# Another order of the passage to the up quads, a load of its own for the root's table, and two 128-column matmuls in place of one behind 512-column products

## The chip, the cores and the metric

The kernel runs on one core of a Trainium2 chip. A core has a matrix engine (TensorE, PE in the profile), a vector engine (VectorE, DVE), a scalar engine (ScalarE, ACT), GpSimd (POOL) and a sync engine (SP) whose queue issues transfers. The metric is the device time of one execution in microseconds, the median of several runs.

## The reference

One layer of a decoder with x of 512 tokens by 1024 (float32) and 256 memory tokens. Cut to what matters:

```python
h = rmsnorm(x, norm_mix_g)
proj = h @ w_in                       # 1024 x 9216
p_a, p_b, q, p_g = split(proj)
y_a = (gb * conv3(gc * v)) @ w_a_out
y_b = silu(layernorm(conv31(u * sigmoid(ug)))) @ w_b_out
y_c = attention(q, rmsnorm(mem) @ w_kv, 4 heads) @ w_att_out
g = sigmoid(p_g + b_gate)             # three gates
x = x + (g0 * y_a + g1 * y_b + g2 * y_c) @ w_o
h = rmsnorm(x, norm_ffn_g)
u = conv3(h @ w_up); gt, up = split(u)
x = x + (silu(gt) * up) @ w_down      # inner width 2816
return rmsnorm(x, norm_final_g)
```

## The kernel before

**Products.** Each factor in float32 is split into a high part and a low part of the type float32r, and a product is three matmuls: high by high, high by low, low by high. The high part is a copy on ACT (`whi` of a weight, line 481), the low part a subtraction on DVE (`wlo`, line 485).

**Quads.** The large projections are not multiplied block by block but as *quads*: two halves of the 512 tokens, two halves of the 1024 inputs, two groups of columns. Seven products of blocks, with sums and differences before and behind, stand in place of eight. The seven have the numbers 1 to 7. Each product is 24 matmuls of 256 columns (`multiply`, line 662). Its moving operand is one of seven forms of the activations, by `OPERAND`: b00, b10 and b11 are blocks themselves, t4 to t7 sums of blocks. A form is a pair of tiles, `fb00h` and `fb00l` for instance, of four 128 x 256 pieces. In form t4 the first three pieces lie in the tiles `ft4h` and `ft4l`, and the fourth in a tile of its own, `ft4x`, that starts at another offset in memory. Product 4 goes through the pieces in the order 0, 1, 2, 3 for the first 128 output columns and 3, 2, 1, 0 for the second, so the pieces of `ft4x` stand together.

The forms are made for three activations: "h" (the normed x, `high` and `low`, lines 582 and 587), "y" (the output of branch b before w_b_out, `y_parts`, lines 1367 and 1372, made in two halves e = 0 and 1) and "h2" (the normed x of the second half). A quad keeps its sums in PSUM banks "a", "b" and "c". They are read by the jobs r1 to r7 (lines 685 to 715): reads r1, r4, r5 and r6 are on ACT, r2, r3 and r7 on DVE. The read r4 of a quad is the last use of its bank "a".

**Other work of PE.** Between the quads stand products of 512 columns in the same three parts (`product`, lines 432 to 434): values, attention and its output, the merging of branches, wo, and the down projection. There are also transposes (128 columns, lines 1155 and 1756), sums by a column of ones (line 791) and rows (line 800).

**Order.** PE's order is written out by hand as a list `seq`. `beside` (line 1890 and on) says what goes behind which product of a quad: behind product 6 of gate (1, 1) the sums for the layer norm of branch b and a part of a merge, behind its product 7 the layer norm's rows (`pe_rows("v", ...)`) and the rest of the merge, and behind its product 3 the two quads "mq 0" and "mq 1" of w_b_out, product by product in turn. Then come the products of wo, "a b f c d e g" (seven again, in two halves i = 0, 1 each), with `pe_transpose_rows(i)` ahead of each half of "g". Then the 11 up quads, with the transposes of rows 2 and 3 between their first products, and the down projection.

The other engines' orders are made by a planner. Every piece of work is a `job` with an engine, a cost, jobs that must come before it and buffers that it takes; the tables `LATER` and `AHEAD` shift kinds of jobs in time. The planner has no job for the loading of an activation table on ACT. Where the function changes to one of another table, the load is put ahead of the activation that needs it (1.28 us each, lines 1325, 1492, 1743). Each engine then works in program order.

**From wo to the up quads.** When the last of wo's products for a row of 128 tokens is in PSUM, DVE adds it to x (`add_row`, line 1730). ACT squares the row (`row_square`, 1737) and takes the root (`row_root`, 1743). DVE takes the reciprocal and scales (`row_norm`, 1747 and 1748). PE transposes (1756), and ACT and DVE make the forms "h2". Rows 0 and 1 are finished by product "e" of wo, rows 2 and 3 by "g".

Of the kernel before, what the change touches and what calls it, by code (L numbers as in the profile page):

```python
# [8 lines left out]
F32 = mybir.dt.float32  # L9
F32R = mybir.dt.float32r  # L10
AF = mybir.ActivationFunctionType
ALU = mybir.AluOpType
# [304 lines left out]
def hybrid_block_kernel(  # L317
# [42 lines left out]
    def name(s):  # L360
        uid[0] += 1
        return f"{s}_{uid[0]}"
# [181 lines left out]
    def form_tile(act, key):  # L544

        n = 3 if key == "t4" else 4
        t = [forms.tile([P, n, HALF], F32R, tag=key + s, name=name("f" + key + s)) for s in "hl"]
        form[act, key] = [[x[:, k, :] for k in range(n)] for x in t]
        if key == "t4":
            gap = (256 - SHIFT) // 4  # L550
            last = forms.tile([P, gap + 2 * HALF], F32R, tag="t4x", name=name("ft4x"))
            for i in range(2):
                form[act, key][i].append(last[:, gap + i * HALF : gap + (i + 1) * HALF])
            form[act, key, "views"] = [[x, y[3]] for x, y in zip(t, form[act, key])]
        else:
            form[act, key, "views"] = [[x] for x in t]
        return form[act, key, "views"]
# [6 lines left out]
    def form_jobs(act, blk, ready, sources=()):  # L564
# [10 lines left out]

        def pieces(t, views):
            return [t] if len(views) == 1 else [t[:, :3, :], t[:, 3, :]]

        def high(key, src):
            hi = form_tile(act, key)[0]  # L580
            for h, x in zip(hi, pieces(src(), hi)):
                nc.scalar.copy(h, x)

        def low(key, src):
            hi, lo = form[act, key, "views"]
            for h, l, x in zip(hi, lo, pieces(src(), hi)):
                nc.vector.tensor_tensor(l, x, h.bitcast(F32), op=ALU.subtract)

# [24 lines left out]
    def quad_loads(q, w, col0, col1, by_dma=False, take=("wf",), after=(), lows=()):  # L613
# [34 lines left out]
        split_job((q, 4), r, 4, 256, [("ld", r)], lo_from=low(4, 1, 1))  # L648

    def multiply(q, f, act):  # L650
        if f in (1, 2, 5):
            make(("bank", q, BANK_OF[f]))
        ps = halves(("bank", q, BANK_OF[f]))
        (w_hi, w_lo), (hi, lo) = w_units.pop((q, f)), form[act, OPERAND[f]]
        for c in range(2):
            at = slice(c * P, (c + 1) * P)
            for i in range(4):
                k = 3 - i if f == 4 and c else i
                first = f in (1, 2, 5) and i == 0 and c == 0
                again = not (f in (1, 2, 5) and c == 0)  # L660
                for n, (w, a) in enumerate(((w_hi, hi), (w_hi, lo), (w_lo, hi))):
                    nc.tensor.matmul(  # L662
                        ps[:, c, :], w[:, k, at], a[k], start=first and n == 0,
                        stop=i == 3 and n == 2, skip_group_check=again,
                    )

# [685 lines left out]
    def y_parts(key, e, src, after, use):  # L1352
        last = next(f for f in OPERAND if OPERAND[f] == key)

        def pieces(views):

            if len(views) == 1:
                return [(slice(0, 2), views[0][:, 2 * e : 2 * e + 2, :])]
            if e == 0:
                return [(slice(0, 2), views[0][:, :2, :])]  # L1360
            return [(slice(0, 1), views[0][:, 2:3, :]), (slice(1, 2), views[1].unsqueeze(1))]

        def high():
            if e == 0:
                form_tile("y", key)
            for at, h in pieces(form["y", key, "views"][0]):
                nc.scalar.copy(h, src()[:, at, :])

        def low():
            hi, lo = form["y", key, "views"]  # L1370
            for (at, h), (_, l) in zip(pieces(hi), pieces(lo)):
                nc.vector.tensor_tensor(l, src()[:, at, :], h.bitcast(F32), op=ALU.subtract)  # L1372

        hk, lk = ("fh", "y", key, e), ("fl", "y", key, e)
        job(hk, "ACT", actv(512), high,
            after + [(("gate", 1, 1), last)] + ([("fh", "y", key, 0)] if e else []), use=use)
        job(lk, "DVE", dve(512), low, [hk], use=use)
        form_ready.setdefault(("y", key), []).append(lk)
        return lk
# [355 lines left out]
    def row_square(t):  # L1735
# [3 lines left out]
        )  # L1739

    def row_root(t):
        r = column(SS_X + t, 1)
        nc.scalar.activation(r, r, AF.Sqrt, bias=eps, scale=1.0 / D)
# [48 lines left out]
    for t in range(NT):  # L1792
# [4 lines left out]
            take=[(("xnorm", t), "sb")], use=[("x1", t)])  # L1797
        job(("xroot", t), "ACT", 0.3, lambda t=t: row_root(t), [("xsquare", t)])
        job(("xnorm", t), "DVE", 1.40, lambda t=t: row_norm(t),
# [72 lines left out]
    for do in (  # L1872
# [38 lines left out]
        (GATE[1, 1], 6): lambda: (  # L1911
            pe_squares("v", ("csq", 0), NT, SEQ, [("var", "fold")], SEQ), pe_merge(0, 3, (0,))),
        (GATE[1, 1], 7): lambda: (pe_rows("v", R_V, NT), pe_merge(0, 3, (1,))),
        (GATE[1, 1], 3): lambda: [
# [7 lines left out]
    for p in WO:  # L1922
        for i in range(2):
            if p == "g":
                pe_transpose_rows(i)
            pe_wo(p, i)

# [391 lines left out]
```

## Time and profile before

| | us |
|---|---|
| median of 3 runs | 934.01 (931.47 to 934.22) |
| the profiled execution | 931.92 |
| its span, from first to last instruction | 930.2 |
| PE busy | 915.1 (98%) |
| DVE busy | 848.1 (91%) |
| ACT busy | 686.0 (74%) |
| PE's waits with a named releaser, in sum | 6.8 |

The table is from the page of the profile. Engine times overlap, so they do not add up. A matmul's record is longer than the distance to the next one: the matmuls are pipelined, and what counts is from start to start. In the trace a row shows its start, its length, engine, line, operation, output and inputs (buffer numbers left out), and in brackets the idle time before it and what ended it. "x8" groups eight instructions in a row.

### The profile page before, as it was taken

What the parts mean: (1) busy time and instruction counts of PE and PEld (TensorE: products, weight loads), DVE (VectorE), ACT (ScalarE), POOL (GpSimd) and SP (SyncE); (2) the same over time, 40 slices, a digit from 0 to 9 for tenths busy, and PEclk for the clock granted to TensorE, in tenths of its full rate; (3) what the DMA queues carried; (4) which work ended last, traced back from release to release, by engine and by line L of the source; (5) the groups of instructions that cost most, each with busy time, mean ns of one, the idle gap of its engine ahead of it and who ended that gap; (6) DMA issues with size and microseconds to landing.
All of it is one profiled execution on the core that took longest, in us unless ns stands there. A gap on an engine that the chain in (4) does not pass through costs nothing.

```text
span 930.2 us, 17118 instructions
## 1 busy us (share of the span) xinstructions
PE 915.1 (98%) x6813; PEld 863.5 (93%) x6813; DVE 848.1 (91%) x976; ACT 686.0 (74%) x938; POOL 137.4 (15%) x165
## 2 busy tenths in 40 slices
PE   9999999999999999999999999999999999999996
PEld 8999999999889999999899897799999999988885
DVE  7998999999989999999886999797999889999986
ACT  8577988889978867878767983686766667765665
POOL 0121111000011111120101211111221111002300
PEclk9999999999999999999999999999999999999999
DMA  9999579745688898887868899889999886689952
GB/s 363 382 251 227 123 182 220 166 114 113 165 183 222 204 203 202 215 187 212 181 140 214 199 252 330 206 211 305 278 245 230 201 167 128 169 313 316 248 110 91
DMA packets 55952, 196.91 MB, mean 212 GB/s; under 512 B 6336, under 2 KB 6464, under 8 KB 55872
## 3 DMA queue, kind: packets, MB, share of 16 engines
q0 software_dynamic: 22608, 81.54, 48.4%
q1 hardware_dynamic: 32544, 113.23, 33.5%
q8 instruction: 53, 0.87, 0.4%
q10 hardware_dynamic: 720, 1.06, 0.3%
q14 instruction: 27, 0.22, 0.1%
HBM read 191.60 MB, written 4.19 MB: 211 GB/s over the span
## 4 chain that ended last, share of the span: by engine, by line
PE 83%; issue 7%; DMA 4%; DVE 3%; ACT 1%; POOL 1%; ACTq 0%; POOLq 0%; DVEq 0%
PE bank L662 55%; PE bank L432 6%; PE bank L434 6%; PE bank L433 5%; PE bank L1469 3%; PE bank L1467 3%; PE bank L1468 3%; PE bank L918 2%; DMA wo<-in_w_o 2%; DMA wf<-in_w_b_out 2%; DMA wf<-in_w_up 1%; DVE wlo L485 1%; ACT whi L481 0%; PE bank L1155 0%; POOL whol L502 0%
## 5 line engine op out<-in xcount | busy, mean ns | idle before, releaser
L481 ACT CAST whi<-wf 128x1024 fp32r<-128x1024 f32 x202 | 210.6, 1045 | 92.4 <-PE bank L662 37.5
L485 DVE TENSOR_TENSOR wlo<-wf,whi 128x1024 fp32r<-128x1024 f32 (+1 forms) x196 | 235.8, 1210 | 23.5 <-ACT whi L481 23.2
L1227 ACT ACTIVATE tp<-u,pk 128x510 f32<-128x510 f32 (+22 forms) x184 | 119.0, 705 | 4.5 <-DVE acc L1234 2.0
L1234 DVE TENSOR_TENSOR acc<-acc,tp 128x988 f32<-128x988 f32 (+22 forms) x92 | 109.0, 1186 | 8.8 <-ACT tp L1227 7.4
L619 POOL DMA_DIRECT2D wf<-in_w_in x48 | 42.9, 908 | 230.7 <-DVE wlo L485 167.4
L662 PE MATMUL bank<-fb10h,whi 128*128 128x256 f32 x248 | 69.0, 278 | 1.7 <-ACT g L712 1.3
L662 PE MATMUL bank<-fb10l,whi 128*128 128x256 f32 x248 | 68.6, 277 | 0.6 <-DVE fb10l L1372 0.6
L662 PE MATMUL bank<-ft6h,whi 128*128 128x256 f32 x248 | 68.7, 277 | 0.1
L662 PE MATMUL bank<-fb11h,wlo 128*128 128x256 f32 x248 | 68.6, 277 | 0.1
L662 PE MATMUL bank<-ft6l,whi 128*128 128x256 f32 x248 | 68.7, 277 | 0.0
L662 PE MATMUL bank<-fb00h,whi 128*128 128x256 f32 x248 | 68.7, 277 | 0.0
L662 PE MATMUL bank<-ft5l,whi 128*128 128x256 f32 x248 | 68.7, 277 | 0.0
L662 PE MATMUL bank<-fb11h,whi 128*128 128x256 f32 x248 | 68.7, 277 | 0.0
L662 PE MATMUL bank<-ft7h,whi 128*128 128x256 f32 x248 | 68.7, 277 | 0.0
L662 PE MATMUL bank<-ft7l,whi 128*128 128x256 f32 x248 | 68.7, 277 | 0.0
L662 PE MATMUL bank<-ft7h,wlo 128*128 128x256 f32 x248 | 68.7, 277 | 0.0
L662 PE MATMUL bank<-fb00l,whi 128*128 128x256 f32 x248 | 68.6, 277 | 0.0
L662 PE MATMUL bank<-fb00h,wlo 128*128 128x256 f32 x248 | 68.6, 277 | 0.0
L662 PE MATMUL bank<-ft6h,wlo 128*128 128x256 f32 x248 | 68.6, 277 | 0.0
L662 PE MATMUL bank<-ft5h,wlo 128*128 128x256 f32 x248 | 68.6, 277 | 0.0
L662 PE MATMUL bank<-ft5h,whi 128*128 128x256 f32 x248 | 68.6, 277 | 0.0
L662 PE MATMUL bank<-fb11l,whi 128*128 128x256 f32 x248 | 68.5, 276 | 0.0
(416 smaller groups left out, 3151.7 us busy)
## 6 DMA issues: line engine op xcount, KB each, us to landing
wf<-in_w_in SPq DMA_DIRECT2D x52, 512.0 KB, 5.1
wf<-in_w_in POOLq DMA_DIRECT2D x48, 512.0 KB, 6.2
wf<-in_w_up POOLq DMA_DIRECT2D x31, 512.0 KB, 7.3
wf<-in_w_up SPq DMA_DIRECT2D x29, 512.0 KB, 7.9
wf<-in_w_down SPq DMA_DIRECT2D x15, 512.0 KB, 4.5
wf<-in_w_att_out SPq DMA_DIRECT2D x8, 512.0 KB, 3.8
wf<-in_w_a_out SPq DMA_DIRECT2D x8, 512.0 KB, 3.7
wf<-in_w_b_out SPq DMA_DIRECT2D x8, 512.0 KB, 6.4
```

Of the source, the lines that this page charges most:

```text
L432: nc.tensor.matmul(ps, s_hi, w_hi, start=start, stop=False, skip_group_check=again)
L433: nc.tensor.matmul(ps, s_hi, w_lo, start=False, stop=False, skip_group_check=again)
L434: nc.tensor.matmul(ps, s_lo, w_hi, start=False, stop=stop, skip_group_check=again)
L481: nc.scalar.copy(parts[0], src())
L485: nc.vector.tensor_tensor(lo, src(), hi.bitcast(F32), op=ALU.subtract)
L619: nc.gpsimd.dma_start(out=tiles[key], in_=block(w, col[c], k), accum_op=ALU.add)
L662: nc.tensor.matmul(ps[:, c, :], w[:, k, at], a[k], start=first and n == 0, stop=i == 3 and n == 2, skip_group_check=again,)
L1227: nc.scalar.activation(two(("tp", p, s))[:, j, s:], two(("u", p))[:, j, : SEQ - s], AF.Copy, scale=weight(j),)
L1234: nc.vector.tensor_tensor(a, a, two(("tp", p, s))[:, :, s:], op=ALU.add)
L1467: nc.tensor.matmul(ps, w_hi[:, i, at], hi, start=first, stop=False)
L1468: nc.tensor.matmul(ps, w_hi[:, i, at], lo, start=False, stop=False)
L1469: nc.tensor.matmul(ps, w_lo[:, i, at], hi, start=False, stop=last)
```

## The change

- The form t4 becomes a tile like the others; `ft4x` and the reversed order of its pieces go. `y_parts` and the form jobs copy and subtract t4 in one instruction each.
- In `multiply`, the first matmul of a product becomes two of 128 columns each, with the same weights, if the work before it in PE's order is long (512 columns: values, attention's weighted sum, merge, wo, mean, down) and the work behind it is another product of a quad. This holds for eight products.
- A job "roots" loads the table of the square root on ACT. It comes after the twelve sigmoids; the roots of the rows come after it.
- The rows of branch b's layer norm move from behind product 7 of gate (1, 1) to behind product 6, after the part of a merge there.
- In wo, both transposes of rows 0 and 1 stand between the two halves of "g", where one stood ahead of each half.

The planner works anew from this. On SP one load of w_o, of x and of w_up each comes at another place; POOL's order stays. ACT has the read r4 of gate (1, 1) behind the table load and two sigmoids of that time, one more weight copy and both halves of `ft4h`, which it stood ahead of. ACT has the square of row 2, a weight copy and then the root of row 2. DVE's order in the passage from wo to up stays.

```diff
--- before.py
+++ after.py
@@ -543,17 +543,9 @@
 
     def form_tile(act, key):
 
-        n = 3 if key == "t4" else 4
-        t = [forms.tile([P, n, HALF], F32R, tag=key + s, name=name("f" + key + s)) for s in "hl"]
-        form[act, key] = [[x[:, k, :] for k in range(n)] for x in t]
-        if key == "t4":
-            gap = (256 - SHIFT) // 4
-            last = forms.tile([P, gap + 2 * HALF], F32R, tag="t4x", name=name("ft4x"))
-            for i in range(2):
-                form[act, key][i].append(last[:, gap + i * HALF : gap + (i + 1) * HALF])
-            form[act, key, "views"] = [[x, y[3]] for x, y in zip(t, form[act, key])]
-        else:
-            form[act, key, "views"] = [[x] for x in t]
+        t = [forms.tile([P, 4, HALF], F32R, tag=key + s, name=name("f" + key + s)) for s in "hl"]
+        form[act, key] = [[x[:, k, :] for k in range(4)] for x in t]
+        form[act, key, "views"] = [[x] for x in t]
         return form[act, key, "views"]
 
 
@@ -573,18 +565,13 @@
         def sum_t7():
             nc.vector.tensor_tensor(b(0, 1), b(1, 1), b(0, 1), op=ALU.subtract)
 
-        def pieces(t, views):
-            return [t] if len(views) == 1 else [t[:, :3, :], t[:, 3, :]]
-
         def high(key, src):
-            hi = form_tile(act, key)[0]
-            for h, x in zip(hi, pieces(src(), hi)):
-                nc.scalar.copy(h, x)
+            ((hi,), _) = form_tile(act, key)
+            nc.scalar.copy(hi, src())
 
         def low(key, src):
-            hi, lo = form[act, key, "views"]
-            for h, l, x in zip(hi, lo, pieces(src(), hi)):
-                nc.vector.tensor_tensor(l, x, h.bitcast(F32), op=ALU.subtract)
+            (hi,), (lo,) = form[act, key, "views"]
+            nc.vector.tensor_tensor(lo, src(), hi.bitcast(F32), op=ALU.subtract)
 
         def parts(key, src, after, use):
             if act == "h" and key in MEM_LAST:
@@ -647,22 +634,32 @@
         fetch_job(r, block(w, col1, 1), after=after, take=take)
         split_job((q, 4), r, 4, 256, [("ld", r)], lo_from=low(4, 1, 1))
 
+    def long_rows(key):
+
+        return key[0] in ("V", "o", "merge", "pd") or key[0] == "wo" and key[1] not in WO_WHOLE or key[1] == "mean"
+
     def multiply(q, f, act):
         if f in (1, 2, 5):
             make(("bank", q, BANK_OF[f]))
         ps = halves(("bank", q, BANK_OF[f]))
         (w_hi, w_lo), (hi, lo) = w_units.pop((q, f)), form[act, OPERAND[f]]
+        here = seq.index((q, f))
+        halved = long_rows(seq[here - 1]) and isinstance(seq[here + 1][0], tuple)
         for c in range(2):
             at = slice(c * P, (c + 1) * P)
-            for i in range(4):
-                k = 3 - i if f == 4 and c else i
-                first = f in (1, 2, 5) and i == 0 and c == 0
-                again = not (f in (1, 2, 5) and c == 0)
+            for k in range(4):
+                first = f in (1, 2, 5) and k == 0 and c == 0
+                again = halved or not (f in (1, 2, 5) and c == 0)
                 for n, (w, a) in enumerate(((w_hi, hi), (w_hi, lo), (w_lo, hi))):
-                    nc.tensor.matmul(
-                        ps[:, c, :], w[:, k, at], a[k], start=first and n == 0,
-                        stop=i == 3 and n == 2, skip_group_check=again,
-                    )
+                    cols = [slice(0, HALF)]
+                    if halved and (c, k, n) == (0, 0, 0):
+                        cols = [slice(0, HALF // 2), slice(HALF // 2, HALF)]
+                    for part in cols:
+                        nc.tensor.matmul(
+                            ps[:, c, part], w[:, k, at], a[k][:, part],
+                            start=first and n == 0 and part.start == 0,
+                            stop=k == 3 and n == 2, skip_group_check=again,
+                        )
 
     def multiply_job(q, f, act, unit=True):
         bank = ("bank", q, BANK_OF[f])
@@ -1352,24 +1349,16 @@
     def y_parts(key, e, src, after, use):
         last = next(f for f in OPERAND if OPERAND[f] == key)
 
-        def pieces(views):
-
-            if len(views) == 1:
-                return [(slice(0, 2), views[0][:, 2 * e : 2 * e + 2, :])]
-            if e == 0:
-                return [(slice(0, 2), views[0][:, :2, :])]
-            return [(slice(0, 1), views[0][:, 2:3, :]), (slice(1, 2), views[1].unsqueeze(1))]
+        at = slice(2 * e, 2 * e + 2)
 
         def high():
             if e == 0:
                 form_tile("y", key)
-            for at, h in pieces(form["y", key, "views"][0]):
-                nc.scalar.copy(h, src()[:, at, :])
+            nc.scalar.copy(form["y", key, "views"][0][0][:, at, :], src())
 
         def low():
-            hi, lo = form["y", key, "views"]
-            for (at, h), (_, l) in zip(pieces(hi), pieces(lo)):
-                nc.vector.tensor_tensor(l, src()[:, at, :], h.bitcast(F32), op=ALU.subtract)
+            hi, lo = (t[:, at, :] for (t,) in form["y", key, "views"])
+            nc.vector.tensor_tensor(lo, src(), hi.bitcast(F32), op=ALU.subtract)
 
         hk, lk = ("fh", "y", key, e), ("fl", "y", key, e)
         job(hk, "ACT", actv(512), high,
@@ -1738,6 +1727,9 @@
             tiles["xnorm", t], tiles["x1", t], AF.Square, accum_out=column(SS_X + t, 1)
         )
 
+    job("roots", "ACT", 1.28, lambda: nc.scalar.preload_act_table_set("sqrt_and_others"),
+        [("sigmoid", br, m) for br in range(3) for m in range(4)])
+
     def row_root(t):
         r = column(SS_X + t, 1)
         nc.scalar.activation(r, r, AF.Sqrt, bias=eps, scale=1.0 / D)
@@ -1795,7 +1787,7 @@
             out=x1_kept[t], in_=tiles["x1", t]), both, LOAD_LATENCY, use=[("x1", t)])
         job(("xsquare", t), "ACT", actv(1024), lambda t=t: row_square(t), both,
             take=[(("xnorm", t), "sb")], use=[("x1", t)])
-        job(("xroot", t), "ACT", 0.3, lambda t=t: row_root(t), [("xsquare", t)])
+        job(("xroot", t), "ACT", 0.3, lambda t=t: row_root(t), [("xsquare", t), "roots"])
         job(("xnorm", t), "DVE", 1.40, lambda t=t: row_norm(t),
             [("xroot", t), "ldg"], use=[("xnorm", t), ("x1", t), ("gffn",)])
         for i in range(2):
@@ -1909,8 +1901,9 @@
         (GATE[0, 1], 3): lambda: [pe_merge(0, m) for m in range(3)],
         (GATE[1, 0], 6): lambda: pe_mean("mu"),
         (GATE[1, 1], 6): lambda: (
-            pe_squares("v", ("csq", 0), NT, SEQ, [("var", "fold")], SEQ), pe_merge(0, 3, (0,))),
-        (GATE[1, 1], 7): lambda: (pe_rows("v", R_V, NT), pe_merge(0, 3, (1,))),
+            pe_squares("v", ("csq", 0), NT, SEQ, [("var", "fold")], SEQ), pe_merge(0, 3, (0,)),
+            pe_rows("v", R_V, NT)),
+        (GATE[1, 1], 7): lambda: pe_merge(0, 3, (1,)),
         (GATE[1, 1], 3): lambda: [
             multiply_job(("mq", q), f, "y") for f in (1, 5, 2, 6, 7, 4, 3) for q in range(2)],
     }
@@ -1920,10 +1913,11 @@
             beside[q, f]()
 
     for p in WO:
-        for i in range(2):
-            if p == "g":
-                pe_transpose_rows(i)
-            pe_wo(p, i)
+        pe_wo(p, 0)
+        if p == "g":
+            for t in range(2):
+                pe_transpose_rows(t)
+        pe_wo(p, 1)
 
 
     ENDS = [slice(0, 256), slice(256, 512)]
```

## The prediction

> **What bounds the kernel now.** I read the page first: the busy share of each engine and the chain that ended last.
>
> ```profile
> span 930.2 us, 17118 instructions
> ...
> PE 915.1 (98%) x6813; PEld 863.5 (93%) x6813; DVE 848.1 (91%) x976; ACT 686.0 (74%) x938; POOL 137.4 (15%) x165
> ...
> PE 83%; issue 7%; DMA 4%; DVE 3%; ACT 1%; POOL 1%; ACTq 0%; POOLq 0%; DVEq 0%
> PE bank L662 55%; PE bank L432 6%; PE bank L434 6%; PE bank L433 5%; PE bank L1469 3%; PE bank L1467 3%; PE bank L1468 3%; PE bank L918 2%; DMA wo<-in_w_o 2%; DMA wf<-in_w_b_out 2%; DMA wf<-in_w_up 1%; DVE wlo L485 1%; ACT whi L481 0%; PE bank L1155 0%; POOL whol L502 0%
> ```
>
> TensorE (PE) sets the time: it is busy 98% of the span, and over half of the chain is line 662, the 256-column matmuls of the quads. So a change can act in two ways: on the step from one matmul to the next, and on the few waits that PE has. My sum is about the profiled execution: 931.92 us, of which 930.2 are span. It stands 2.1 us below the median of the runs, 934.01.
>
> The steps are read from stretches of whole products (24 matmuls each). Columns: stretch, its length, PE's busy time and the matmuls that touch it (a few more than start in it), granted clock, DMA share, GB/s.
>
> ```profile
> 192.93:198.57 5.64, 5.64 (x49) 1.00 0.54 143
> 225.33:236.62 11.29, 11.29 (x97) 1.00 0.22 72
> 285.60:299.72 14.12, 14.12 (x122) 1.00 0.82 222
> 299.72:438.72 139.00, 139.00 (x1227) 1.00 0.84 200
> 381.48:392.36 10.88, 10.88 (x99) 1.00 1.04 220
> 392.36:395.12 2.76, 2.76 (x27) 1.00 1.00 384
> 474.65:485.94 11.29, 11.29 (x97) 1.00 0.63 144
> 500.46:503.29 2.83, 2.83 (x25) 1.00 0.66 114
> 509.20:512.02 2.82, 2.82 (x26) 1.00 0.97 155
> 591.87:595.13 3.26, 1.39 (x10) 1.00 1.04 261
> 595.13:598.55 3.42, 3.42 (x9) 0.50 0.06 12
> 603.02:608.68 5.66, 5.66 (x49) 1.00 1.04 258
> ```
>
> There are two paces at full clock. 381.48 to 392.36 is four products, 2.72 us each (113.3 ns a matmul). 285.60 to 299.72 is five products, 2.824 each (117.7 ns). The slow pace starts where a product follows 512-column work, and it lasts until something shakes it off. The t4 product is what shakes it off here: 285.60 starts a slow stretch of five, the fifth is t4, and 299.72 is fast again. The t4 product itself, in a fast stretch, takes 2.76 (392.36 to 395.12), 0.04 above the others. That is the fourth block lying in a tile of its own, ft4x.
>
> **The change, part by part.**
>
> *t4 in one tile.* 22 of the 31 t4 products run at the 2.76 of that row; they lose the extra 0.04: -0.88 us. The others lie in slow stretches, priced next. The joined copies and subtractions on ACT and DVE (three instructions fewer on ACT, two on DVE) lie beside PE and count nothing.
>
> *Two 128-column matmuls for one.* The condition (long rows before, another quad product behind) holds at eight products. In the times of the profile before, they start at 43.48, 62.60, 192.93, 225.33, 285.60, 474.65, 509.20 and 603.02. The price of a 128-column matmul comes from the transposes:
>
> ```profile
> 177.43 1.04 PE L1155 MATMUL bank<-ident,pr 128*128 128x128 f32 x8
> 178.22 0.36 PE L662 MATMUL bank<-fb10h,whi 128*128 128x256 f32 x1
> 178.42 0.28 PE L662 MATMUL bank<-fb10l,whi 128*128 128x256 f32 x1
> ```
>
> Eight of them and one 256-column matmul take 0.99 us from first start to the start after: (0.99 - 0.113) / 8 = 0.11 each, almost what 256 columns take. Two for one cost 0.22 - 0.113 = 0.107, eight times: +0.86 us. Bounds: 0 at the least, if the second half hides; at the most two halves at the half-clock pace of the 0.50 row (0.22 each), which gives 8 x 0.33 = 2.6. I take the transposes, the same number of columns.
>
> The Trainium skill ("TensorE: Matmul & The Clock Gate", section "Back-to-back issue gap") gives about 81 ns for a sustained matmul of 128 columns; by that the eight halvings would cost 8 x 0.049 = 0.39 us, and the whole sum would be 0.47 lower. The row shows 110 ns, so I go by the row.
>
> *What the halving is worth* if it shakes the slow pace off as the transposes and t4 do. Excess of the stretches over 2.72 a product: 192.93 two products 0.20; 225.33 four 0.41; 285.60 five 0.52; 474.65 four 0.41; 509.20 one 0.10; 603.02 two 0.22: -1.86. At 43.48 and 62.60 nothing is won. A product followed by long work again is not halved and stays slow. The product at 500.46 is slow (2.83); after the change the 128-column rows of the layer norm stand before it: -0.11. Bounds: -1.97 to 0. I take the full, since t4 and transposes both end a slow stretch whenever they meet one. Steps together: -0.88 + 0.86 - 1.97 = -2.0 us.
>
> *Layer-norm rows before the t7 product of gate (1,1).* The rows get to PE one product (2.83) earlier, so the swish of branch b, on ACT, comes earlier, and what waits for it. But ACT's order around it changes too:
>
> ```profile
> 523.06 1.28 ACT L1325 ACT_TABLE_LOAD   x1
> 524.36 1.52 ACT L1325 ACTIVATE acc<-acc,pk 128x512 f32<-128x512 f32 x2
> ...
> 526.25 0.62 ACT L1367 CAST fb10h<-acc 128x512 fp32r<-128x512 f32 x1
> ...
> 530.66 0.61 ACT L712 ACTIVATE g<-bank 128x512 f32<-128x512 f32 x1
> 531.15 1.05 ACT L481 CAST whi<-wf 128x1024 fp32r<-128x1024 f32 x1
> 532.23 1.28 ACT L1492 ACT_TABLE_LOAD   x1
> 533.52 1.34 ACT L1492 ACTIVATE g<-g,pk 128x512 f32<-128x512 f32 x2
> ```
>
> ```profile
> 526.92 0.38 PE L662 MATMUL bank<-fb10h,whi 128*128 128x256 f32 x1 [0.46 <-ACT fb10h L1367]
> 527.86 0.38 PE L662 MATMUL bank<-fb10l,whi 128*128 128x256 f32 x1 [0.56 <-DVE fb10l L1372]
> ...
> 529.78 0.28 PE L662 MATMUL bank<-fb10h,wlo 128*128 128x256 f32 x1
> 531.32 0.38 PE L662 MATMUL bank<-fb10h,whi 128*128 128x256 f32 x1 [1.26 <-ACT g L712]
> ...
> 546.18 0.39 PE L662 MATMUL bank<-ft4h,whi 128*128 128x256 f32 x1 [0.99 <-DVE y L438]
> ```
>
> The matmul at 531.32 opens product 2 of mq 1. It takes the bank that the read of gate (1,1) product 4 (line 712) frees. In the new order a table load (1.28), two sigmoids (1.34), one more weight copy (1.05 at 0.95 a step) and both halves of ft4h (0.5 each) stand ahead of that read on ACT: 4.6 us more. ACT gets there some 2.4 earlier (of the 2.83; the swish chain has other work in it). So it ends at 531.27 + 4.6 - 2.4 = 533.5, and PE, freed of most of the waits of 0.46 and 0.56, is ready near 529.0. One wait of about 4.6 stands in place of four; with the restart after each they cost some 4.0 (3.27 of waits, 0.1 for the longer first record and 0.1 for its slow step at each). The wait at 546.18 goes too, for its operands have 4 us more. Net +0.6 us; bounds -1.5 (ACT gains the full 2.83 and overlaps better) and +3 (it gains nothing).
>
> *From wo to the up quads.* Now:
>
> ```profile
> 593.06 1.06 PE L1756 MATMUL bank<-ident,xnorm 128*128 128x128 f32 x8 [1.03 <-DVE cols L1747]
> 594.96 0.67 PE L432 MATMUL bank<-whi,mgh 128*128 128x512 f32 x1 [0.84 <-DVE x L1730]
> ```
>
> ```profile
> 589.81 1.28 ACT L1743 ACT_TABLE_LOAD   x1
> 591.11 0.48 ACT L1743 ACTIVATE cols<-cols,eps 128x1 f32<-128x1 f32 x2
> ```
>
> ```profile
> 591.63 1.28 DVE L1748 SCALAR_TENSOR_TENSOR xnorm<-x,cols,gffn 128x1024 f32<-128x1024 f32 x1
> ...
> 594.23 1.28 DVE L1730 TENSOR_TENSOR x<-x,bank 128x512 f32<-128x512 f32 x2
> ```
>
> The load of the root's table moves out to behind the last sigmoid, where ACT has time beside PE. The roots come 1.28 earlier, so does DVE's row of work, and the sums that the first half of wo g needs end at 594.9 - 1.28 = 593.6. That half starts there instead of 594.96 (-1.3), but the first transposes, which stood before it (0.8), now follow: -0.5. Its own wait grows to about 1.6. Nothing is gained if DVE is late by other work (0). The squares of rows 2 and 3 come behind the second half, and a weight copy (1.05) stands between square 2 and its root: about +1.0 at the transposes of row 2, which today wait for nothing; bounds 0 and +1.3. Net +0.5.
>
> *The loads.* One load of w_o, one of x and one of w_up change places in SP's queue by a place; POOL's order stays. PE has no wait for a load in this region, so I count 0, up to +0.5.
>
> *The clock.* The rows 591.87 and 595.13 show a cost: PE busy 1.39 of 3.26 us, then 3.42 at clock 0.50, in which half of 3.42 = 1.7 us are lost. The new order packs 2.7 us of 512-column work straight behind the wait, so I expect this slow stretch gone (-1.7). But the wait of 4.6 us at mq is longer than such a stretch, and there I expect one (+1.7). Net 0, bounds -1.7 and +1.7.
>
> The Trainium skill ("TensorE: Matmul & The Clock Gate", section "What's actually happening") says that the clock halves after an idle window of about 3.4 us, which runs free of the kernel. Taken strictly, waits of 1.03 and 0.84 would not have done it; the row shows that they did, with transposes between them. By that rule the wait at mq would do it if a whole window falls inside.
>
> **Sum.** -2.0 (steps) + 0.6 (mq) + 0.5 (wo to up) + 0 (clock) = -0.9: 931.0 for an execution like the profiled one, 933.1 against the median; I say 933.0.
>
> **Rivals.**
> 1. *No new slow stretch of the clock, and ACT's late read comes sooner.* For it: four waits of 0.46 to 1.26 close together kept the clock at 1.00. Against: 4.6 us is far longer. Then -1.7 and about -1: 930.3.
> 2. *Both slow stretches.* The wait before wo g is one of 1.6 us and may still lower the clock there: +1.7, 934.7, with +1 more if row 2's transposes are late by the bound.
> 3. *The halving does not shake off the slow pace (slower).* Then the t4 products no longer do either, and one passage slows everything up to the next other work. The row 299.72:438.72 is 51 products without a break; at 0.104 more each that is +5.3, and the shorter stretches behind 485.94 and 512.02 give +0.9. Without the gain of 1.97 the change is +6.2 - 0.88 + 0.86 + 1.1 = +7.3: 941.3. It decides where the products behind 285.60 do not come back to 2.72. For it: nothing in the trace is an ordinary 128-column matmul behind 512 columns; the transposes are another operation. Against: t4 and the transposes both end the slow pace, and the halving too breaks the even row of 256 columns.
> 4. *The up stage turns slow at a wait,* with no t4x to end it. It happens now: the matmuls of one product there last 281 ns and not 276, the sign of the slow pace, between two short waits.
>
> ```profile
> L662 PE MATMUL bank<-fb11h,whi x8: 276/276/276, 638.1 to 640.5; 128*128 128x256 f32 x8
> L662 PE MATMUL bank<-fb11h,whi x7: 281/281/281, 649.7 to 651.9; 128*128 128x256 f32 x7
> ```
>
> The 155 us that follow, to 807, are 57 products; 57 x 0.104 is +6; I count this with rival 3.
>
> **How the numbers follow.** Chances: forecast 0.38 (own range 930.8 to 935.3), rival 1 0.22, rival 2 0.18, rivals 3 and 4 0.22. The bound for no change is 0.3%, 2.8 us: below 931.2 faster, above 936.8 slower. Faster: 0.12 from the forecast, 0.20 from rival 1, 0.01 from rival 2: 0.33. Slower: 0.21 from rivals 3 and 4, 0.06 from rival 2 and late work, 0.03 from the forecast: 0.30. The rest, 0.37, is the same. The range, 929 to 941, leaves out a tenth at either end.
>
> **What would show it.** Right: products behind the halved ones at 2.72 for a whole quad, t4 at 2.72; the halved product at 2.83; one PE wait of 4 to 5 us by the read of gate (1,1) at the second product of mq 1, with a clock of 0.5 behind it; the first half of wo g waiting 1.6 us and clock 1.00 there; a wait near 1 us at row 2's transposes. Wrong: products at 2.82 in long stretches (rival 3), no wait at mq, or the clock at 0.5 in both places.

## The result and the profile after

The changed kernel is slower. The median is 933.44 us against 931.88 (20 runs of each), 0.17% more; the mean, which the longest executions raise, is 0.3% more: ratio 1.0032 with a 95% interval of 1.0020 to 1.0045. The median of before in these runs is 2.1 us below that of the three runs shown earlier, so the 931.92 of its profiled execution was a typical time after all.

The runs of the changed kernel fall into two groups with nothing between: 13 from 931.53 to 933.92 (median 933.11), called *short* below, and 7 from 938.71 to 940.27 (median 939.29), called *long*. The kernel before has one group, 931.04 to 934.22. The profiled execution of the changed kernel, 932.52, is a short one.

From its page, the busy times and the chain:

```profile
span 930.7 us, 17121 instructions
...
PE 914.0 (98%) x6821; PEld 863.9 (93%) x6821; DVE 848.6 (91%) x973; ACT 685.9 (74%) x935; POOL 137.1 (15%) x165
...
PE 84%; issue 7%; DMA 4%; DVE 2%; ACT 2%; POOL 1%; SPq 0%; ACTq 0%; POOLq 0%; DVEq 0%
```

PE is still the bound. Its four longest waits with a named releaser:

```profile
PE bank L658 <- ACT g L709: 4.5, 1, 4.5
PE bank L1748 <- DVE cols L1739: 1.4, 1, 1.4
PE bank L1859 <- POOL ident masks.py:199: 1.4, 1, 1.4
PE bank L432 <- DVE x L1719: 1.0, 1, 1.0
```

One long wait at mq (line 658 behind the read at line 709, 712 before) has taken the place of four short ones. The wait at the transposes of row 2 (line 1748) is new. The stretches that answer to those shown of before, with the same columns:

```profile
193.44:199.00 5.56, 5.56 (x51) 1.00 0.50 135
225.70:236.70 11.00, 11.00 (x99) 1.00 0.22 79
285.67:299.39 13.72, 13.72 (x122) 1.00 0.79 207
474.05:485.05 11.00, 11.00 (x99) 1.00 0.57 136
532.34:536.20 3.86, 3.86 (x20) 0.56 0.90 255
594.77:598.20 3.43, 3.43 (x18) 1.00 0.87 170
602.13:607.69 5.56, 5.56 (x50) 1.00 1.02 234
610.10:653.47 43.37, 43.37 (x372) 1.00 0.96 254
653.47:797.66 144.19, 144.19 (x1275) 1.00 0.89 206
```

The halving does what was forecast. The five products from 285.67 take 13.72 us: a halved one of 2.84 and four of 2.72; before they took 14.12. The half clock has moved from behind wo g (594.77, now 1.00) to behind the wait at mq (532.34, now 0.56). The row to look at is 610.10:653.47. From the transposes of row 2 on, fifteen products run at the slow pace, 2.83 us each beside the transposes of row 3, with no wait among them (the expectations below say sixteen). The same stage of before, nearly all of it at the fast pace but with short waits, and the rest of the up quads:

```profile
609.47:652.51 43.04, 42.77 (x371) 1.00 0.97 259
652.51:797.08 144.57, 144.57 (x1273) 1.00 0.87 206
```

So the slow stage itself is only 0.33 us longer than that of before. In the changed kernel the pace comes back at 653.47; from there its up quads are 0.38 us shorter than before, because the t4 products no longer pay 0.04 each.

### The profile page after: what moved, and what is told of

It is laid out like the page before. It is cut to its first block, busy times and chain, and to the rows that moved or that the text cites. A ratio compares the mean times of both kernels' runs of the same rounds, so it can differ in the third digit from the quotient of the medians.

```text
span 930.7 us, 17121 instructions
## 1 busy us (share of the span) xinstructions
PE 914.0 (98%) x6821; PEld 863.9 (93%) x6821; DVE 848.6 (91%) x973; ACT 685.9 (74%) x935; POOL 137.1 (15%) x165
## 4 chain that ended last, share of the span: by engine, by line
PE 84%; issue 7%; DMA 4%; DVE 2%; ACT 2%; POOL 1%; SPq 0%; ACTq 0%; POOLq 0%; DVEq 0%
PE bank L658 57%; PE bank L432 5%; PE bank L434 5%; PE bank L433 5%; PE bank L1457 3%; PE bank L1456 3%; PE bank L1458 3%; PE bank L915 2%; DMA wo<-in_w_o 2%; DMA wf<-in_w_b_out 1%; DMA wf<-in_w_v 1%; ACT whi L481 1%; DVE wlo L485 1%; DVE xnorm L1740 0%; PE bank L1152 0%
## 5 line engine op out<-in xcount | busy, mean ns | idle before, releaser
L658 PE MATMUL bank<-fb10h,wlo 128*128 128x256 f32 x248 | 69.4, 280 | 0.0
L658 PE MATMUL bank<-ft6h,whi 128*128 128x256 f32 (+1 forms) x250 | 68.8, 276 | 0.0
L658 PE MATMUL bank<-fb00h,whi 128*128 128x256 f32 (+1 forms) x250 | 68.8, 276 | 0.0
L658 PE MATMUL bank<-ft5h,whi 128*128 128x256 f32 (+1 forms) x251 | 68.7, 276 | 0.0
L658 PE MATMUL bank<-ft4h,whi 128*128 128x256 f32 (+1 forms) x249 | 68.6, 276 | 0.0
L658 PE MATMUL bank<-ft4l,whi 128*128 128x256 f32 x248 | 68.6, 277 | 0.0
L658 PE MATMUL bank<-ft4h,wlo 128*128 128x256 f32 x248 | 68.6, 277 | 0.0
```

The source lines that it names most:

```text
L658: nc.tensor.matmul(ps[:, c, part], w[:, k, at], a[k][:, part], start=first and n == 0 and part.start == 0, stop=k == 3 and n == 2, skip_gr ...
```

## The experiments

Twelve runs. Theory P says that the slow pace in the up quads is what makes the change slower, since ft4x no longer ends it. Theory W says that it is the long waits. *Short* and *long* name groups of executions some 6 us apart in the other kernels too. All medians below are device times. The kernel before, on the same chips, had medians from 931.69 to 931.87, and no execution above 934.33.

### t4 in two tiles again

The changed kernel, with:

```diff
+        n = 3 if key == "t4" else 4
+        if key == "t4":
+            gap = (256 - SHIFT) // 4
+            last = forms.tile([P, gap + 2 * HALF], F32R, tag="t4x", name=name("ft4x"))
...
+                k = 3 - i if f == 4 and c else i
```

> The changed kernel with the fourth piece of t4 in a tile of its own again (ft4x and the reversed order of pieces); halving, roots, rows and the order in wo stay. Theory P (the loss is the slow pace of 117.7 ns a matmul in the up stage, which nothing ends there without ft4x): the up products are back at 2.72 us from the first t4 product on, so the 16 slow products of the profiled execution (16 x 0.107 = 1.7 us) shrink to some 10 or fewer, no execution is near 939, the t4 products take 0.04 more each (31 x 0.04 = 1.2). Median near 932.0 to 932.8, highest under 935. Theory W (the loss is the long waits at mq and at row 2's transposes, and the executions near 939 come from elsewhere): executions near 939 remain, some 6 in 20, and the rest is 1.2 us slower than the changed kernel.

Measured: seven executions from 933.54 to 935.29, median 934.57. No execution is near 939. The rest is some 1.5 us above the short group and outside the 932.0 to 932.8 that theory P gave; ft4x costs about 31 x 0.04 = 1.2, and theory P had hoped for more back. In its trace the up stage still turns slow behind row 2's transposes and comes out of it at the first t4 product:

```profile
611.21:640.43 29.22, 29.22 (x251) 1.00 0.92 211
```

A second slow stretch begins at 655.41, behind a wait of 0.21 us, and ends five products later, again at a t4 product. So ft4x caps the loss, which speaks for P; it does not lower the short group.

### No halving

```diff
-        halved = long_rows(seq[here - 1]) and isinstance(seq[here + 1][0], tuple)
+        halved = False
```

> The changed kernel with one matmul of 256 columns in place of the two of 128 at all eight places (neither halving nor ft4x). If the halving is what keeps the pace: the slow stretch behind 285 runs on for some 50 products (5.3 us), those behind 193, 225, 474 and 508 come back too (about 2 us), less 8 x 0.118 = 0.9 for the halvings: 6 to 7 us above the changed kernel in the same state of the up stage, 938 to 940, up to 946 where the up stage is slow to its end. If the halving does nothing: 0.9 us below the changed kernel.

Measured: median 939.64, four executions from 938.45 to 939.66 and two at 944.8. Without halving and without ft4x the slow pace that starts at 286.75 runs on for 54 products:

```profile
286.75:439.39 152.64, 152.64 (x1297) 1.00 0.84 195
```

That is 2.827 a product. The halving does end the slow pace behind 512 columns. It is worth about 6 us here: the four executions near 939 lie 6.0 above the short group of the changed kernel, the two at 944.8 lie 5.5 above its long group.

### The read r4 ahead of the sigmoids

```diff
             job(("sigmoid", br, m), "ACT", 2 * scaled_act(512), sigmoid,
-                ready_of(("gate", br, m // 2), m % 2) + [("ldp",)], use=[gate])
+                ready_of(("gate", br, m // 2), m % 2) + [("ldp",)]
+                + ([("r4", ("gate", 1, 1))] if (br, m) == (1, 2) else []), use=[gate])
```

> The changed kernel with the third sigmoid of branch b made to wait for the read r4 of gate (1,1), so that a table load (1.28) and two sigmoids (1.34) stand behind that read on ACT and not before it. Theory W: the wait at the second product of mq 1 falls from 4.5 us to about 1.7, and at that length the clock stays at 1.00 behind it (another 1.7): 4 to 4.5 us faster than the changed kernel in the same state of the up stage, 928 to 929. Theory P: the same for the wait, but executions some 6 us longer than the others stay, in a similar share. If the 2.8 us come back elsewhere in the mq quads (the sigmoids are later, and the weighing and merge behind them): 0 to 2 us faster.

Measured: seven short executions (930.72 to 932.22, median 931.33) and five long ones (936.75 to 937.61). The wait at mq fell only from 4.5 to 3.3 us, for ACT now stood idle for a DVE sum ahead of ft4h and had three weight copies ahead of the read; the clock behind was still reduced. The short group gained 1.8 us, the long one stayed 6 us above it. Theory W has its share, but it does not make the two groups.

### The transposes of row 2 one product later

```diff
-(UP[0], 2), "tr2", (UP[1], 1), "tr3", (UP[1], 2),
+(UP[0], 2), (UP[1], 1), "tr2", "tr3", (UP[1], 2),
```

> The changed kernel with the transposes of row 2 one product later, behind the first product of up quad 1, and those of row 3 right behind them. The wait of 1.4 us before the transposes of row 2 goes, or nearly. Theory W: 1 to 1.4 us faster, near 932. Theory P with the wait as the trigger: without a wait there the products behind come out at 2.72, and no execution near 939 is seen; then also the 16 x 0.107 = 1.7 us go, 930 to 931. If transposes may leave the slow pace without a wait: executions near 939 remain.

Measured: median 933.59, seven short (median 932.87) and five long. The wait did not go, it moved to row 3's transposes (1.5 us), and in the trace the slow pace began right behind those. So the run says nothing on transposes without a wait; it shows the start of the slow pace moving with the wait.

### The layer norm's rows back in their place

```diff
-            pe_squares("v", ("csq", 0), NT, SEQ, [("var", "fold")], SEQ), pe_merge(0, 3, (0,)),
-            pe_rows("v", R_V, NT)),
-        (GATE[1, 1], 7): lambda: pe_merge(0, 3, (1,)),
+            pe_squares("v", ("csq", 0), NT, SEQ, [("var", "fold")], SEQ), pe_merge(0, 3, (0,))),
+        (GATE[1, 1], 7): lambda: (pe_rows("v", R_V, NT), pe_merge(0, 3, (1,))),
```

> The changed kernel with the layer norm's rows of branch b behind product 7 of gate (1,1) again, as in the kernel before; all else stays. ACT's order around the read r4 of gate (1,1) is then that of before. If the move of the rows makes the long wait: the wait of 4.5 us and the half clock behind it go, and the four short waits of before (3.3 us) return: 2.0 to 2.5 us below the changed kernel in the same state of the up stage, 930.2 to 931, and 936.5 to 937.5 in the long state. If the wait comes from the other parts too: no change or up to 1 us.

Measured: ten short executions (930.07 to 931.47, median 930.84) and two long (936.49, 937.12). The wait at the read is 1.2 us and the clock from 520 to 560 is 1.00. The move of the rows cost 933.11 - 930.84 = 2.3 us. Behind that wait nine products of the mq quads run at the slow pace. Even so they take as long as in the kernel before, where they run at the fast pace and wait 0.99 us for an operand (first row: rows back; second: before):

```profile
530.73:556.73 26.00, 25.81 (x217) 1.00 0.99 256
531.32:557.26 25.94, 24.95 (x216) 1.00 0.97 257
```

### wo and the root's table as before

```diff
-        pe_wo(p, 0)
-        if p == "g":
-            for t in range(2):
-                pe_transpose_rows(t)
-        pe_wo(p, 1)
+        for i in range(2):
+            if p == "g":
+                pe_transpose_rows(i)
+            pe_wo(p, i)
...
-        job(("xroot", t), "ACT", 0.3, lambda t=t: row_root(t), [("xsquare", t), "roots"])
+        job(("xroot", t), "ACT", 0.3, lambda t=t: row_root(t), [("xsquare", t)])
```

The job "roots" goes too.

> The changed kernel with the order in wo (a transpose ahead of each half of g) and the root's table as in the kernel before; halving, t4 in one tile and the rows' move stay. From the traces the new order gains 2.6 us up to the first up product and loses 1.5 at the transposes of row 2. Theory P (the slow pace in the up stage starts at the products behind the transposes of row 2 that waited): row 2's transposes come without a wait, the products behind them run at 2.72, no or few executions near 939, and the median is at or below the changed kernel's: 930.5 to 932.5. If the slow pace starts without that wait too: 933.5 to 934.5 in the short state, and a share of executions 5 to 6 us longer as in the changed kernel.

Measured: median 932.15, ten short (median 932.06) and two long (937.01, 939.24), though the mq wait of 4.5 us is still there. Row 2's transposes have no wait, and in the trace no up product is slow until the last quad. That is theory P's forecast; the long executions are fewer but not gone.

### Halving behind row 3's transposes

```diff
-        halved = long_rows(seq[here - 1]) and isinstance(seq[here + 1][0], tuple)
+        halved = (long_rows(seq[here - 1]) or seq[here - 1] == ("tr", 3)) and isinstance(seq[here + 1][0], tuple)
```

> The changed kernel with one more halving: the product behind the transposes of row 3 (up quad 1, product 2) begins with two matmuls of 128 columns. Theory P: the slow pace that starts behind the transposes of row 2 ends there; the 14 or so slow products after it (14 x 0.107 = 1.5 us) go, for 0.118, and with them the executions near 939, unless a later short wait brings the pace down again: 931.0 to 931.5, highest under 934. Theory W: no change of the shares, 0.1 us longer.

Measured: six short (931.53 to 933.01) and six long (937.54 to 939.25). The halved product stayed slow, and all behind it:

```profile
613.91:653.68 39.77, 39.77 (x341) 1.00 0.97 256
```

A miss for the cure: in this execution a pair of 128 columns that stands behind eight other 128-column instructions did not bring the pace back.

### The part on the pace alone

The changed kernel with the layer norm's rows, the order in wo and the root's table all as before; the halving and t4 in one tile stay.

> The kernel before with the part on the pace alone: t4 in one tile and the halving at eight places; rows, order in wo and root's table as before. ACT, DVE and PE have the order of before but for that. By the sum of the steps 2.0 us less than before where the up stage is at 2.72: 930.0 with waits as before. With theory P a share of executions has the up stage slow to some later point, up to 6 us longer (up to 936.5), because nothing there ends it.

Measured: six short executions (929.04 to 930.69, median 929.93) and two long (935.74, 936.55). The short group is 1.9 us below the kernel before, as the sum of the steps had it. The profile fell on a long one, and it shows what a long execution of this kernel is:

```profile
613.51:648.00 34.49, 33.69 (x292) 1.00 0.99 267
651.50:809.89 158.39, 158.39 (x1344) 1.00 0.86 196
```

From 651.50 on 56 products take 2.828 us each, to the end of the stage: 56 x 0.108 = 6.0 us. Row 2's transposes had no wait in this execution, so a long one does not need that. What stands in front of 651.50 is a short wait:

```profile
651.00 0.28 PE L658 MATMUL bank<-fb11h,wlo 128*128 128x256 f32 x1
651.50 0.39 PE L658 MATMUL bank<-ft6h,whi 128*128 128x256 f32 x1 [0.22 <-ACT gt L686]
```

### Halving in the kernel before, t4 in two tiles

The kernel before, with the new `multiply` but ft4x and its order of pieces kept.

> The kernel before with the halving alone: t4 keeps its tile ft4x and its order of pieces, the rest is as before. Five or six slow stretches behind 512 columns shrink (1.86 us by the prediction's sum) for 8 x 0.118 = 0.94: 0.9 us below the kernel before, 931.0. Since t4x still ends a slow pace in each up quad, no execution is 4 us or more above the others. If the long executions come from the halving itself: some near 936 to 937.

Measured: median 931.01, 929.90 to 932.12, ratio 0.9990 (0.9981 to 0.9998), no long execution in 11. In its profile, too, the pace turned slow behind a wait in the up quads, at 651.74, and t4 ended it five products later.

### The same with the root's table

```diff
+    job("roots", "ACT", 1.28, lambda: nc.scalar.preload_act_table_set("sqrt_and_others"),
+        [("sigmoid", br, m) for br in range(3) for m in range(4)])
...
+        job(("xroot", t), "ACT", 0.3, lambda t=t: row_root(t), [("xsquare", t), "roots"])
```

> The same with the job for the root's table, in the old order of wo (transposes ahead of each half of g). The roots of rows 0 and 1 come 1.28 us earlier, so the wait of 1.03 before the first transposes goes and that of 0.84 before the first half of g shrinks. If waits that short kept the clock down (0.50 for 3.4 us): another 1.7. Row 2's square and root stay as they were, so no wait at its transposes. Between 1.0 and 3.0 us below the halving alone: 928 to 930. If DVE is late by other work: no change.

Measured: median 929.73, 928.71 to 930.19, ratio 0.9976 (0.9966 to 0.9987), no long execution in 8. It beats both kernels. Without the job and with it, in the old order of wo, the stretch around the first transposes:

```profile
589.00:593.00 4.00, 3.18 (x17) 1.00 1.03 318
593.00:597.00 4.00, 3.17 (x17) 1.00 0.54 126
```

```profile
587.00:591.00 4.00, 4.00 (x19) 1.00 1.05 254
591.00:595.00 4.00, 4.00 (x22) 1.00 0.95 262
```

Both waits are gone, 1.6 us of them, with no change of PE's order.

### Halving product 4 of each up quad

```diff
-        halved = long_rows(seq[here - 1]) and isinstance(seq[here + 1][0], tuple)
+        halved = long_rows(seq[here - 1]) and isinstance(seq[here + 1][0], tuple) or q[0] == "up" and f == 4
```

on the kernel of the part on the pace alone.

> The kernel with the halving and t4 in one tile, rest as before (as in the run of that pair), and product 4 of each up quad halved as well: a matmul pair of 128 columns in a stream of 256. If the pair ends a slow pace anywhere: no long executions, 11 x 0.118 = 1.3 us above the short state of that run, 931.3. If it ends it only behind 512 columns, as the run with the halving behind row 3's transposes suggests: long executions stay (a fifth to a third), 5 to 6 us above the others.

Measured: median 930.88, 929.85 to 931.41, no long execution in 11, where the kernel without these pairs had two in eight. The pair seems to end the slow pace in a stream of 256 columns, as theory P needs. That rests on the times alone. The profiled execution had two slow products in that stage (616.22 to 621.98), but they ended 11 us ahead of the first halved product 4, so the pair did not end them.

### Both transposes later

On the kernel with the rows back:

```diff
-(UP[0], 2), "tr2", (UP[1], 1), "tr3", (UP[1], 2),
+(UP[0], 2), (UP[1], 1), "tr2", (UP[1], 2), "tr3",
```

> The changed kernel with the rows' move undone and the transposes of rows 2 and 3 each one product later (behind products 1 and 2 of up quad 1), where their rows are ready: about 609 and 611 by the trace, for starts near 610 and 614. No wait at row 2's transposes. Theory P with the wait as trigger: the products behind run at 2.72 and 16 x 0.107 = 1.7 us go beside the 1.4 of the wait; product 5 of up quad 0, with its sum t5 of all rows, may now wait about 1 us. Net 1 to 3 us below the run with the rows' move undone, 928.0 to 930.0; fewer long executions, since a later wait can still start one. If the slow pace starts at the transposes without a wait: 930 to 931.

Measured: three short (934.39 to 934.87) and six long (939.36 to 940.62). The wait at row 2's transposes is gone and no product behind them is slow in the trace, as P has it. But the form t5 comes late:

```profile
PE bank L658 <- ACT ft5h L570: 2.9, 1, 2.9
...
PE bank L658 <- DVE ft5l L574: 1.2, 1, 1.2
```

These new waits cost more than the old one, and a stretch at half clock lies over the second of them, which costs some 2.5 us more (half of the 5.00 in which PE is busy; the columns are as before):

```profile
617.75:624.58 6.83, 5.00 (x21) 0.50 0.74 154
```

The forecast of the net, 928.0 to 930.0, was wrong by about 5 us, for it had 1 us for the wait at t5 and nothing for the clock. The share of long executions is the highest of all. The profiled one is short, and its products are fast again once the clock is back, so what makes the others long is not shown.

## Why the prediction was wrong

It forecast a change of -0.9 us, to 933.0 against the median then shown. The median is 933.44, but measured against 20 runs of before the change is +1.6, and +1.2 for the short executions. That 933.0 lies near 933.44 is luck: the base was 2.1 too high, which hid most of a miss of 2.5 in the change. Medians of the short groups split the change into three parts, each to be set against a part of the sum.

| part | forecast | measured | from |
|---|---|---|---|
| steps: t4 in one tile, halving | -2.0 | -1.9 | 929.93 against 931.79 to 931.87 |
| rows of the layer norm, clock at mq | +0.6, +1.7 | +2.3 | 933.11 - 930.84 |
| wo to up, clock behind wo g | +0.5, -1.7 | +0.9 | 930.84 - 929.93 |

**The steps** were right, by size and by place. A halved product takes 0.118 more, against 0.107 from the transposes, and the products behind are at 2.72.

**The rows at mq** were right. The read ends at 532.29, and ACT does stand in the forecast order ahead of it: table load, sigmoids, an extra copy, both halves of ft4h. In order of time:

```profile
524.27 1.28 ACT L1481 ACT_TABLE_LOAD   x1
525.57 1.34 ACT L1481 ACTIVATE g<-g,pk 128x512 f32<-128x512 f32 x2
...
530.16 1.14 ACT L1357 CAST ft4h<-acc 128x512 fp32r<-128x512 f32 x2
...
531.68 0.61 ACT L709 ACTIVATE g<-bank 128x512 f32<-128x512 f32 x1
```

The wait is 4.50 against 4.6, and the half clock follows it. The slow products of the run with the rows back do not disturb the 2.3, for that stretch is as long as in the kernel before (26.00 against 25.94).

**From wo to the up quads** is the step that failed, by 2.1 us: 1.7 of clock that were not gained, and a wait of 1.43 that the sum had at 1.0.

*First, the gain of 1.7 from the clock was no gain of the new order.* The half clock behind wo g was in the one execution of before that was profiled. Between that and the changed kernel's the stretch from the first product of wo to the first up product did shrink by the forecast amount, from 45.76 to 43.57. But in four other kernels with the old order of wo the same part had the clock at 1.00:

```profile
589.78:600.58 10.80, 9.55 (x50) 1.00 0.75 204
```

(from the part on the pace alone; the three others show 1.00 too). Their stretch from wo to up takes 43.8 to 44.2, so the new order gains 0.2 to 0.6 on it and not 2.2. The sum took one execution for the kernel. How often the half clock falls there in the kernel before stays open: it was profiled once, and the four others differ from it by the halving too. Nor is time won ahead of the up quads kept whole. In the run with the halving in the kernel before, the up quads begin 2.1 us earlier than in before (600.95 against 603.02), but the ft6 product at 651.74, behind b11, begins only 0.8 earlier (652.51 in before): waits of 0.88, 0.57 and 0.21 us stand between.

*Second, the sum let the up quads run at 2.72 behind the new wait.* The wait itself was seen (+1.0; it is 1.43):

```profile
609.28 1.06 PE L1748 MATMUL bank<-ident,xnorm 128*128 128x128 f32 x8 [1.43 <-DVE cols L1739]
```

But behind it the pace was slow, in every profiled execution with a wait of 1.3 us or more there: the changed kernel, and the runs with t4 in two tiles, without halving (slow ahead of the wait already), with r4 first, with the rows back and with the halving behind row 3. Right behind these transposes it was at 2.72 in the kernels without that wait: wo as before, the pace alone, halves in the kernel before with and without roots, and product 4 halved. That is rival 4 of the prediction: "The up stage turns slow at a wait, with no t4x to end it". It named the price, up to +6 us. The 7 long executions of 20 have the size of its case: 939.29 - 933.11 = 6.2, and the 56 products of the long profile cost 6.0. No long execution of the changed kernel itself was profiled, so this is not shown.

In the short executions the slow pace comes back to fast at 653, and there it costs next to nothing. From row 2's transposes to that point the changed kernel (first row) takes as long as the one with wo as before (second row), whose products are fast but wait, 0.61 us for a weight and 0.22 at a read among others:

```profile
609.28:653.47 44.19, 44.19 (x377) 1.00 0.97 253
607.83:652.10 44.27, 43.44 (x379) 1.00 0.99 273
```

So the 15 x 0.107 = 1.6 us of slow steps stand in place of waits and do not come on top of them. What the up quads of a short execution lose is the wait: from the first up product to that point the changed kernel takes 51.34, the one with wo as before 49.83. The prediction counted rival 4 in one chance with rival 3, and did not join it with the wait of +1.0 that its own sum put there.

**The other rivals.** Rival 3, the halving without effect, was wrong; the run without halving gave nearly the time that it named for that case, 939.6 against its 941.3. Rivals 1 and 2 did not come in the profiled execution: there is one slow stretch of the clock, where the forecast had it. The wait ahead of the first half of wo g is 1.04 and not 1.6.

**The base.** The forecast added 2.1 us to come from the profiled execution to a median of three runs. With 20 runs the profiled time is the median, and that conversion was only noise.

**Open.** Why a wait leaves PE at one pace or the other is not settled. The ft6 product behind b11 shows it. Behind a wait of 0.21 or 0.22 us at its start the slow pace began there in three profiles (the pace alone, 651.50; halves in the kernel before, 651.74; t4 in two tiles, 655.41), and did not in two others (wo as before, product 4 halved). In the changed kernel (653.47) and in the five other profiles that came to it slow, without a wait that the profile lists, the pace turned fast there, behind steps of 0.137 to 0.285 us in place of 0.118.

## What to carry to other kernels

A stretch of one execution that is worth counting (a half clock, a slow pace) must be found in several executions before its end is put down as a gain. A slow pace must not be priced as steps times count where the engine would otherwise wait: measure between the same two instructions in both kernels. Where something small in a kernel, here a tile of its own for one block that costs 0.04 us a product, resets a state of PE, look for all the places at which that state can start before taking it away: the passages behind 512 columns got a new reset, the waits in the up quads did not. Moving the load of the root's table to an earlier place on ACT gave 1.3 us without touching PE; reordering PE around the same wait gave the wait to another row.

## What was unexpected of the hardware

A stream of 256-column matmuls of this type has two steady paces at full clock, 113.3 and 117.7 ns, and stays in the one it has for over 150 us. It turned slow behind a wait of only 0.22 us in one profile, and with the same wait stayed fast in another. The times of one and the same program fall into two groups 6 us apart, which is what 56 products at the slow pace add. Two matmuls of 128 columns in place of one end the slow pace behind 512 columns (the five products of 13.72 us), but did not behind eight transposes (39.77 us for 14 products). The first of such a pair starts its second after 0.06 us when it stands behind 512 columns: the price of the pair is in the matmul behind it, and the sum, 0.118, is near the 0.107 that transposes gave.
